# A mixture-of-experts encoder layer on one core: TensorE's order written out by hand from the third expert on

## The chip, the cores and the metric

One NeuronCore of a Trainium2 chip runs the whole program. The metric is the time of one execution on the device in microseconds (us), the median of the runs shown; a profiled execution is a run of its own. TensorE (PE in the profile, with its weight loads as PEld), VectorE (DVE), ScalarE (ACT), GpSimd (POOL) and SyncE (SP) each work through a queue of their own in order and wait for each other on semaphores.

## The reference

One encoder layer on 1024 tokens of width 1024 in float32: attention, a residual with layer norm, then a mixture of experts with 32 experts, four per token, and a second layer norm. What the change touches is the experts:

```
logits = x @ router_w + router_b
gates  = softmax(top 4 of the logits)
for each expert e, over the rows (tokens) that chose it:
    h = rows @ w_gate_up[e] + b_gate_up[e]              # 1024 -> 2048
    a = clamped_swiglu(h)                               # 2048 -> 1024
    y = a @ w_down[e]                                   # 1024 -> 1024
    out[token] += gate * (y + b_down[e])
x = layer_norm(alpha * x + out)
```

## The kernel before, in words

The attention stage (0 to about 530 us) and the router (to about 660 us) stand ahead of the experts and are not touched. The experts take most of the rest, to about 2045 us.

Experts run in an order e = 0 to 31. Each has a block of 128 rows; 18 of them, e = 1 to 8 and the even ones from 10 to 28 (`ovf(e)`, line 1132), have 32 overflow rows besides. The loop at the end of the stage calls, for each e, `gate_up(e)` (line 1212) and then `down(e - 1)` (line 1273), so the second product of an expert comes after the first product of the next.

A **weight piece** is a tile of 128 x 2048 float32 that SyncE fetches: eight for gate-up (called g0 to g7 below), four for down (d0 to d3). Products keep near float32 precision by splitting both factors into a high and a low part and adding three matmuls (`mm3`, all at line 55). So each piece is cast on ScalarE to `wh` (`prep_hi`, line 618) and its remainder `wl` is taken on VectorE (`prep_lo`, line 623), and TensorE then runs 12 matmuls of 128 x 512 on it. The tiles `wh` and `wl` come from a pool of three: the cast of piece n+3 can't start before TensorE has done its last read of piece n.

The stationary factor is the rows, transposed. For each expert `turn` (line 1144) lets TensorE transpose into the PSUM tile `tp` (line 1147), and `split` (lines 63 and 64) copies it out: ScalarE the high part, VectorE the low part, both reading `tp`. There is **one** `tp` tile (`ps_t`, `bufs=1`), so the next transposes wait until both have read it. The parts are, in one call of `gate_up(e)`: `turn_a(e-1, 0)` and `(e-1, 1)`, two halves of the activations of the expert before (`tpa`, four transposes each); `turn_a(e-1, 2)`, its overflow rows (`tpao`, two transposes, copied out by ScalarE alone), if it has any; and `turn_x(e+1, ...)`, the same three for the rows of the next expert (`tpx`, `tpx`, `tpxo`). `between` says after which piece of the gate-up each part stands in the program.

Overflow rows use TensorE in four strips of 32 columns: after piece g3 and after g7 a block of 16 float32 matmuls each (`go`), after d3 another (`yq`). The bias of gate-up is added by matmuls of `sel` with `b3` in bfloat16, four of 128 x 512 for `gu` and four of 32 x 512 for `go`, at the head of `gate_up`.

What sets the order: instructions are placed on each engine by a scheduler that works from estimated times, except inside `manual_schedule`, where the named engine keeps the order of the program. Before, TensorE is under it in `down` of experts with overflow rows only (line 1283). So in `gate_up` the scheduler moves transposes and biases about.

```python
            tp = ps_t.tile([P, 4, P], F32, tag="tp", name=f"tp{nm}")
            for c in range(nk):
                nc.tensor.transpose(tp[:, c, :], src[:, c * P:(c + 1) * P], ident)
            if lo is None:
                nc.scalar.copy(hi, tp[:, 0:nk, :])
            else:
                split(hi, lo, tp[:, 0:nk, :])
```

Of the kernel before, what the change touches and what calls it, by code (L numbers as in the profile page):

```python
# [20 lines left out]
P = 128  # L21
# [9 lines left out]
OVF = 32  # L31
# [14 lines left out]
def trunk_kernel(ctx: ExitStack, tc: tile.TileContext, x, w_qkv, q_norm, k_norm, w_o,  # L46
# [7 lines left out]
    def mm(o, lhsT, rhs, start=True, stop=True):  # L54
        nc.tensor.matmul(o, lhsT=lhsT, rhs=rhs, start=start, stop=stop)  # L55
# [525 lines left out]
    b3 = keep.tile([P, 2 * D], BF16, name="b3")  # L581
# [4 lines left out]
    sel = keep.tile([P, NE], BF16, name="sel")  # L586
# [461 lines left out]
    with tc.tile_pool(name="moex", bufs=1, side="right", reuse_waits="tile") as mx, \  # L1048
# [83 lines left out]
        def ovf(e):  # L1132
            return 1 <= RANK[e] <= NO
# [78 lines left out]
        def gate_up(e, between):  # L1212
            gus = [ps_g.tile([P, D], F32, tag=f"gu{h}", name=f"gu{e}_{h}") for h in range(2)]
            gu = [gus[n // 2][:, n % 2 * 512:(n % 2 + 1) * 512] for n in range(4)]
            if ovf(e):
                go = ps_o.tile([P, 512], F32, tag="o", name=f"go{e}")
            for n in range(4):
                sl = slice(n * 512, (n + 1) * 512)
                mm(gu[n], sel[:, e:e + 1].to_broadcast([P, P]), b3[:, sl], True, False)
            for n in range(4 if ovf(e) else 0):  # L1220
                mm(go[n * OVF:(n + 1) * OVF], sel[:, e:e + 1].to_broadcast([P, OVF]),
                   b3[:, n * 512:(n + 1) * 512], True, False)
            act[e], part, whole = swiglu(gus, D, e)
            by_cols = e in (0, NE - 1)
            later = []
            for k in range(KD - 2 if by_cols else KD):
                fetch(ci[0] + len(order))
                prep(ci[0] + 3)
                hi, lo, w = wts.pop((e, "g", k))
                xh, xl = xT[e][0][:, k, :], xT[e][1][:, k, :]  # L1230
                for n in range(4):
                    sl = slice(n * 512, (n + 1) * 512)
                    mm3(gu[n], xh, xl, hi[:, sl], lo[:, sl], False, k == KD - 1)
                later.append((k, w))
                if k % 4 == 4 - 1:
                    for kk, w in later if ovf(e) else ():
                        j, hf = divmod(kk, 2)
                        ts = slice(j * OVF, (j + 1) * OVF)
                        for n in range(4):
                            mm(go[n * OVF:(n + 1) * OVF], xoT[e][:, hf, ts], w[:, n * 512:(n + 1) * 512],  # L1240
                               False, kk == KD - 1)
                    later.clear()
                ci[0] += 1
                if k in between:
                    between[k]()
            if by_cols:

                end = []
                for k in range(KD - 2, KD):
                    fetch(ci[0] + len(order))  # L1250
                    prep(ci[0] + 3)
                    end.append((k, wts.pop((e, "g", k))))
                    ci[0] += 1
                for n in range(4):
                    sl = slice(n * 512, (n + 1) * 512)
                    for k, (hi, lo, w) in end:
                        mm3(gu[n], xT[e][0][:, k, :], xT[e][1][:, k, :], hi[:, sl], lo[:, sl], False, k == KD - 1)
                    if n == 0:
                        for k in (KD - 2, KD - 1):
                            if k in between:  # L1260
                                between[k]()
                    if n == 1:
                        part(0)
                part(1)
            else:
                whole()
            xT.pop(e)
            if ovf(e):
                xoT.pop(e)
                acto[e], _, whole = swiglu([go], 256, f"o{e}")  # L1270
                whole()

        def down(e, between={}):
            y = ys.pop(e, None) or mp.tile([P, D], F32, tag="y", bufs=2, name=f"y{e}")
            yp = ps_g.tile([P, D], F32, tag="gu0", name=f"yp{e}") if e == NE - 1 else \
                ps_y.tile([P, D], F32, tag="y", name=f"yp{e}")
            if ovf(e):
                yq = ps_o.tile([P, 512], F32, tag="o", name=f"yq{e}")
            ah, al = actT[e]
            later = []  # L1280
            in_turn = ExitStack()
            if ovf(e):
                in_turn.enter_context(tc.manual_schedule(engines={mybir.EngineType.PE}))
            for c in range(KD // 2):
                fetch(ci[0] + len(order))
                prep(ci[0] + 3)
                hi, lo, w = wts.pop((e, "d", c))
                for j in range(2):
                    k = 2 * c + j
                    for n in range(2):  # L1290
                        sl = slice(j * D + n * 512, j * D + (n + 1) * 512)
                        mm3(yp[:, n * 512:(n + 1) * 512], ah[:, k, :], al[:, k, :], hi[:, sl], lo[:, sl],
                            k == 0, k == KD - 1)
                later.append((c, w))
                if c == KD // 2 - 1:
                    for cc, w in later if ovf(e) else ():
                        ts = slice(cc * OVF, (cc + 1) * OVF)
                        for j in range(2):
                            for n in range(2):
                                sl = slice(j * D + n * 512, j * D + (n + 1) * 512)  # L1300
                                m = 2 * j + n
                                mm(yq[m * OVF:(m + 1) * OVF], actoT[e][:, j, ts], w[:, sl],
                                   cc == 0, cc == KD // 2 - 1)
                    later.clear()
                ci[0] += 1
                if c in between:
                    between[c]()
            in_turn.close()
            nc.scalar.mul(y, yp, gm_s[:, e:e + 1])  # L1309
            nc.gpsimd.indirect_dma_start(  # L1310
                out=fd, out_offset=bass.IndirectOffsetOnAxis(ap=mi[:, e:e + 1], axis=0),
                in_=y, in_offset=None, bounds_check=T + P - 1, oob_is_err=True, compute_op=ALU.add)
            if e == NE - 1:

                idle = ps_y.tile([P, D], F32, tag="y", name="idle")
                for r in range(22):
                    mm(idle[:, 0:512], ah[:, KD - 1, :], hi[:, 0:512])
            if not ovf(e):
                return
            H2 = 2 * OVF  # L1320
            ya = mp.tile([H2, 512], F32, tag="ya", bufs=1, name=f"ya{e}")
            nc.scalar.mul(ya, yq[H2:P], go_s[H2:P, e:e + 1])
            yo = mp.tile([H2, 512], F32, tag="yo", bufs=2, name=f"yo{e}")
            nc.vector.scalar_tensor_tensor(yo, yq[0:H2], go_s[0:H2, e:e + 1], ya, ALU.mult, ALU.add)
            nc.gpsimd.indirect_dma_start(
                out=fd2, out_offset=bass.IndirectOffsetOnAxis(ap=toh[:, e:e + 1], axis=0),
                in_=yo, in_offset=None, bounds_check=2 * (T + P) - 1, oob_is_err=True, compute_op=ALU.add)

        fetch(8)
        for e in range(NE):  # L1330
            between = {}
            if e > 0:
                for part in range(3):
                    between[part] = lambda part=part: turn_a(e - 1, part)
            if e + 1 < NE:
                if e == 0:
                    between[X1] = lambda: [turn_x(1, part) for part in range(3)]
                else:
                    for part in range(3):
                        between[(4 if e == 2 else 3) + part] = lambda part=part: turn_x(e + 1, part)  # L1340
            if e == 0:
                with tc.manual_schedule(engines={mybir.EngineType.DVE}):
                    slots(lambda: prep_lo(2))
            gate_up(e, between)
            if e == 1:
                list_blocks()
            if e + 2 < NE:
                gather_x(e + 2)
                gather_o(e + 2)
            if e == NE - 1:  # L1350
                between = {1 + part: lambda part=part: turn_a(NE - 1, part) for part in range(3)}
                down(e - 1, between)
            elif e > 0:
                down(e - 1)
        down(NE - 1)

    es_w.close()

# [161 lines left out]
```

## Time and profile before

| | us |
|---|---|
| median of 3 runs | 2085.25 (2083.95 to 2086.52) |
| the profiled execution's own time | 2086.0 |
| its span, first to last instruction | 2084.1 |
| TensorE busy in the span | 2031.2 |
| mean granted clock of TensorE | 0.993 |

Of a timeline row the first number is the start in us from the span's start, the second the duration. Matmuls are pipelined: a duration is longer than the distance to the next start, and it is the distances between starts that add up to the time. `LDWEIGHTS` on PEld loads the stationary factor of the matmul of the same name. In square brackets stands how long the engine was idle before, and what ended it. Buffer numbers are left out of names, so `tpx` is every `tpx`.

### The profile page before, as it was taken

Reading aid. Unit: us, or ns where it says so; the run is one execution under the profiler, and the core shown is the slowest. Engines: PE = TensorE matmul, PEld = TensorE weight load, DVE = VectorE, ACT = ScalarE, POOL = GpSimd, SP = SyncE. Lnnn points to the kernel's source line nnn. Section 1 sums busy time; section 2 is a strip of 40 time slices with the busy share of each in tenths; the row PEclk is TensorE's granted clock in tenths of the full one; section 3 lists DMA queues with packets and bytes.
Section 4 is the critical chain, followed back from the end, with each engine's and each line's share of the span. In section 5 each row is a group of like instructions: output and inputs, shape, how many; then the busy total and the mean of one; then the engine's idle time right before and its main releaser. Section 6 shows DMA issues by size and latency. Waiting matters only on the chain. (4 is left out here: it accounts for less than half of the span.)

```text
span 2084.1 us, 27850 instructions
## 1 busy us (share of the span) xinstructions
PE 2031.2 (97%) x10179; PEld 1374.0 (66%) x10179; DVE 1623.8 (78%) x1778; ACT 1292.0 (62%) x1566; POOL 534.8 (26%) x373
## 2 busy tenths in 40 slices
PE   8999999999997999999999999999999999999997
PEld 6774444444675666666667767767777677677774
DVE  6658778887888787776777878888778788887894
ACT  5656655565554656665666767667667676676774
POOL 1216676766134311121111102111011121011000
PEclk9999999999998999999999999999999999999999
DMA  5216000000545678778888988978989789789885
GB/s 173 71 61 178 31 31 21 31 21 11 201 153 205 261 287 304 279 284 295 291 300 333 361 304 317 366 288 349 334 319 372 291 330 355 284 345 340 325 319 182
DMA packets 106350, 500.38 MB, mean 240 GB/s; under 512 B 16002, under 2 KB 17027, under 8 KB 73443
## 3 DMA queue, kind: packets, MB, share of 16 engines
q1 hardware_dynamic: 87360, 447.02, 55.6%
q0 software_dynamic: 16000, 50.90, 8.9%
q8 instruction: 81, 1.33, 0.3%
q10 hardware_dynamic: 2850, 0.66, 0.2%
q14 instruction: 59, 0.48, 0.1%
HBM read 457.05 MB, written 41.49 MB: 239 GB/s over the span
## 5 line engine op out<-in xcount | busy, mean ns | idle before, releaser
L55 PE MATMUL gu<-wh,xTh 128*128 128x512 f32 x1024 | 415.0, 405 | 1.0 <-ACT xTh L63 1.0
L55 PE MATMUL gu<-wh,xTl 128*128 128x512 f32 x1024 | 409.9, 400 | 0.0
L55 PE MATMUL gu<-wl,xTh 128*128 128x512 f32 x1024 | 402.0, 394 | 0.2 <-DVE wl L623 0.2
L1310 POOL DMA_INDIRECT fd<-y,mi x32 | 79.1, 2473 | 655.6 <-ACT y L1309 655.6
L450 ACT ACTIVATE pt<-st 128x512 f32<-128x512 f32 x256 | 150.6, 597 | 134.9 <-PE st L55 109.6
L55 PEld LDWEIGHTS gu<-wh,xTh 128*128 128x128 f32 x1024 | 193.4, 189 | 42.5 <-ACT xTh L63 1.7
L55 PEld LDWEIGHTS gu<-wl,xTh 128*128 128x128 f32 x1024 | 193.1, 189 | 40.1 <-DVE wl L623 0.8
L55 PEld LDWEIGHTS gu<-wh,xTl 128*128 128x128 f32 x1024 | 193.5, 189 | 39.0 <-issue 3.6
L454 POOL TENSOR_TENSOR acc<-acc,pt 128x512 f32<-128x512 f32 x152 | 201.2, 1324 | 48.7 <-ACT pt L450 39.7
L55 PE MATMUL yp<-wl,aTh 128*128 128x512 f32 x512 | 204.3, 399 | 0.4 <-DVE wl L623 0.4
L55 PE MATMUL yp<-wh,aTh 128*128 128x512 f32 x512 | 201.6, 394 | 0.0
L55 PE MATMUL yp<-wh,aTl 128*128 128x512 f32 x512 | 199.7, 390 | 0.0
L440 DVE TENSOR_REDUCE nm<-sc 128x1 f32<-128x1024 f32 x124 | 150.4, 1220 | 29.2 <-PE sc L55 28.2
L55 PE MATMUL po<-pt,vn 128*64 128x512 f32 x512 | 135.7, 615 | 2.1 <-DVE ot L475 2.1
L609 POOL DMA_INDIRECT xg<-xd,mi x32 | 53.5, 1671 | 289.8 <-PE tpx L1147 281.7
L55 PE MATMUL qkv<-wh,xT 128*128 128x512 f32 x384 | 123.5, 402 | 2.6 <-ACT xT L63 1.4
L55 PE MATMUL st<-qs,kT_hi 128*128 128x512 f32 x256 | 116.6, 456 | 3.4 <-ACT pt L450 3.2
L55 PEld LDWEIGHTS yp<-wh,aTh 128*128 128x128 f32 x512 | 96.1, 188 | 33.5 <-ACT act L1191 14.2
L55 PEld LDWEIGHTS st<-qs,kT_hi 128*128 128x128 f32 x256 | 48.0, 187 | 97.7 <-ACT pt L450 66.9
L55 PEld LDWEIGHTS yp<-wl,aTh 128*128 128x128 f32 x512 | 96.3, 188 | 22.0 <-DVE wl L623 1.2
L55 PEld LDWEIGHTS yp<-wh,aTl 128*128 128x128 f32 x512 | 96.1, 188 | 19.6
L55 PE MATMUL st<-q,kT_lo 128*128 128x512 f32 x256 | 102.3, 400 | 0.6 <-DVE q L158 0.6
(523 smaller groups left out, 4209.4 us busy)
## 6 DMA issues: line engine op xcount, KB each, us to landing
w0g<-in_expert_w_gate_up SPq DMA_DIRECT2D x8, 1024.0 KB, 8.3
w1g<-in_expert_w_gate_up SPq DMA_DIRECT2D x8, 1024.0 KB, 7.7
w2g<-in_expert_w_gate_up SPq DMA_DIRECT2D x8, 1024.0 KB, 9.4
w3g<-in_expert_w_gate_up SPq DMA_DIRECT2D x8, 1024.0 KB, 7.0
w4g<-in_expert_w_gate_up SPq DMA_DIRECT2D x8, 1024.0 KB, 6.5
w5g<-in_expert_w_gate_up SPq DMA_DIRECT2D x8, 1024.0 KB, 6.7
w6g<-in_expert_w_gate_up SPq DMA_DIRECT2D x8, 1024.0 KB, 7.4
w7g<-in_expert_w_gate_up SPq DMA_DIRECT2D x8, 1024.0 KB, 7.8
```

The lines of the kernel that those rows point to most:

```text
L55: nc.tensor.matmul(o, lhsT=lhsT, rhs=rhs, start=start, stop=stop)
L440: nc.vector.tensor_reduce(nms[n][:, m:m + 1], sc.pop((n, m)), AX.X, ALU.max, negate=True)
L450: nc.scalar.activation(pts[n, k], st, AF.Exp)
L454: (nc.vector if k == 7 or n == NG - 1 or n == NG - 2 and k > 3 else nc.gpsimd).tensor_tensor(accs[n], pts[n, 0] if k == 1 else accs[n], pt ...
L609: return nc.gpsimd.indirect_dma_start(out=xg[e], out_offset=None, in_=xd, in_offset=bass.IndirectOffsetOnAxis(ap=mi[:, e:e + 1] if rows is ...
L1310: nc.gpsimd.indirect_dma_start(out=fd, out_offset=bass.IndirectOffsetOnAxis(ap=mi[:, e:e + 1], axis=0), in_=y, in_offset=None, bounds_chec ...
```

## The change

It puts TensorE under `manual_schedule` from the end of `gate_up(1)` to the end of `down(31)`, so that its instructions keep the program's order from expert 2 on. It moves the three parts of each `turn` in the program: from after pieces g0, g1, g2 (activations) to after g0, g2, g3, and from g3, g4, g5 (next rows; g4, g5, g6 in expert 2) to g4, g6, g7. And it moves the four `go` biases from the head of `gate_up` to just ahead of the first `go` block, behind g3. The work is the same, instruction by instruction.

```diff
-            for n in range(4 if ovf(e) else 0):
-                mm(go[n * OVF:(n + 1) * OVF], sel[:, e:e + 1].to_broadcast([P, OVF]),
-                   b3[:, n * 512:(n + 1) * 512], True, False)
             act[e], part, whole = swiglu(gus, D, e)
...
                 if k % 4 == 4 - 1:
+                    for n in range(4 if ovf(e) and k == 4 - 1 else 0):
+                        mm(go[n * OVF:(n + 1) * OVF], sel[:, e:e + 1].to_broadcast([P, OVF]),
+                           b3[:, n * 512:(n + 1) * 512], True, False)
                     for kk, w in later if ovf(e) else ():
...
-            in_turn = ExitStack()
-            if ovf(e):
-                in_turn.enter_context(tc.manual_schedule(engines={mybir.EngineType.PE}))
             for c in range(KD // 2):
...
-            in_turn.close()
...
         fetch(8)
+        in_turn = ExitStack()
         for e in range(NE):
             between = {}
             if e > 0:
-                for part in range(3):
-                    between[part] = lambda part=part: turn_a(e - 1, part)
+                for k, part in zip((0, 2, 3) if e > 1 else range(3), range(3)):
+                    between[k] = lambda part=part: turn_a(e - 1, part)
             if e + 1 < NE:
                 if e == 0:
                     between[X1] = lambda: [turn_x(1, part) for part in range(3)]
                 else:
-                    for part in range(3):
-                        between[(4 if e == 2 else 3) + part] = lambda part=part: turn_x(e + 1, part)
+                    for k, part in zip((4, 6, 7) if e > 1 else (3, 4, 5), range(3)):
+                        between[k] = lambda part=part: turn_x(e + 1, part)
...
             if e == 1:
                 list_blocks()
+
+                in_turn.enter_context(tc.manual_schedule(engines={mybir.EngineType.PE}))
...
         down(NE - 1)
+        in_turn.close()
```

On TensorE, in `gate_up(21)`, around the second half of the activations of expert 20 (`tpa20_1`; `wh250` and `wl250` are piece g2, `wh251` and `wl251` g3). Before:

```order
L55 MATMUL gu21_1_13317<-wl250_13328,xTh_21_13114 128x512
L55 MATMUL gu21_1_13317<-wh250_13326,xTh_21_13114 128x512
L1147 MATMUL tpa20_1_13370<-ident_70,act20_12998 128x128 x4
L55 MATMUL gu21_1_13317<-wh250_13326,xTl_21_13115 128x512
L55 MATMUL gu21_1_13317<-wl250_13328,xTh_21_13114 128x512
```

And now:

```order
L55 MATMUL gu21_1_13280<-wh250_13289,xTl_21_13096 128x512
L55 MATMUL gu21_1_13280<-wl250_13291,xTh_21_13095 128x512
L1147 MATMUL tpa20_1_13351<-ident_70,act20_12957 128x128 x4
L55 MATMUL gu21_0_13279<-wh251_13317,xTh_21_13095 128x512
L55 MATMUL gu21_0_13279<-wh251_13317,xTl_21_13096 128x512
```

Before, these transposes stand behind seven of the twelve matmuls of g2; now they stand behind all twelve. The overflow transposes `tpao20` stood behind seven matmuls of g3 and stand behind its twelfth now, with no other transposes between, and `tpxo22` likewise moves from within g6 to the end of g7, one piece behind `tpx22_1`, which moves from within g5 to the end of g6.

On ScalarE at the same place, the casts of g3 (`wh251`) to g6 (`wh254`) and the copies out of `tp` (`aTh`, and `aoT` for the overflow rows). Before:

```order
L618 CAST wh251_13354<-w21g3_13166 128x2048
L63 CAST aTh_20_13342<-tpa20_0_13345 128x512
L618 CAST wh252_13379<-w21g4_13184 128x2048
L63 CAST aTh_20_13342<-tpa20_1_13370 128x512
L618 CAST wh253_13411<-w21g5_13240 128x2048
L1149 COPY aoT20_13344<-tpao20_13395 128x256
L618 CAST wh254_13439<-w21g6_13258 128x2048
```

And now:

```order
L618 CAST wh251_13317<-w21g3_13122 128x2048
L63 CAST aTh_20_13305<-tpa20_0_13308 128x512
L618 CAST wh252_13335<-w21g4_13147 128x2048
L618 CAST wh253_13370<-w21g5_13203 128x2048
L63 CAST aTh_20_13305<-tpa20_1_13351 128x512
L618 CAST wh254_13392<-w21g6_13221 128x2048
L1149 COPY aoT20_13307<-tpao20_13386 128x256
```

The copy of the second half stood ahead of the cast of g5 and stands behind it now. VectorE follows: `aTl` of the second half stood ahead of `wl253` and stands behind it. At `tpx22_1` the same happens with the cast of piece d1 of expert 20 (`wh257`, `wl257`): it stands ahead of the copies of `tpx22_1` now. This is so in every odd `gate_up` from 9 to 29.

## Rows read from the trace of the kernel before

**Rows 1.** The page: TensorE over the span, and its granted clock in 40 slices.
```profile
PE 2031.2 (97%) x10179; PEld 1374.0 (66%) x10179; DVE 1623.8 (78%) x1778; ACT 1292.0 (62%) x1566; POOL 534.8 (26%) x373
...
PEclk9999999999998999999999999999999999999999
```

**Rows 2.** Stretch, length, busy of PE, PEld, DVE, ACT, POOL; PE clock; DMA share; GB/s.
```profile
1500.00:1600.00 100.00, 100.00 (x512) 73.42 (x510) 81.39 (x55) 68.42 (x51) 15.39 (x7) 1.00 0.90 338
```

**Rows 3.** Waits of the weight loads, 740 to 2045: total us, times, longest us.
```profile
PEld tpa L1147 <- DVE aTl L64: 9.9, 30, 0.5
PEld tpx L1147 <- DVE xTl L64: 7.2, 13, 3.2
```

**Rows 4.** TensorE's timeline, expert 19: transposes at the end of a piece (g0).
```profile
1501.96 0.39 PE L55 MATMUL gu<-wl,xTh 128*128 128x512 f32 x1
1502.19 0.60 PE L1147 MATMUL tpa<-ident,act 128*128 128x128 f32 x4
1502.55 0.48 PE L55 MATMUL gu<-wh,xTh 128*128 128x512 f32 x1
1502.86 0.40 PE L55 MATMUL gu<-wh,xTl 128*128 128x512 f32 x1
```

**Rows 5.** The same timeline: transposes within a piece (g2).
```profile
1506.76 0.39 PE L55 MATMUL gu<-wh,xTh 128*128 128x512 f32 x1
1507.05 0.66 PE L1147 MATMUL tpa<-ident,act 128*128 128x128 f32 x4
1507.46 0.48 PE L55 MATMUL gu<-wh,xTl 128*128 128x512 f32 x1
1507.77 0.39 PE L55 MATMUL gu<-wl,xTh 128*128 128x512 f32 x1
```

**Rows 6.** Timeline of all engines, expert 19, from the transposes behind g3 to the next.
```profile
1511.67 1.91 ACT L618 CAST wh<-w19g 128x2048 fp32r<-128x2048 f32 x1 [0.56 <-PE gu L55]
1511.71 0.60 PE L1147 MATMUL tpx<-ident,xg 128*128 128x128 f32 x4
...
1513.48 0.58 ACT L63 CAST xTh<-tpx 128x512 fp32r<-128x512 f32 x1
...
1513.61 2.29 DVE L623 TENSOR_TENSOR wl<-w19g,wh 128x2048 fp32r<-128x2048 f32 x1 [0.71 <-ACT wh L618]
...
1515.82 0.68 DVE L64 TENSOR_TENSOR xTl<-tpx,xTh 128x512 fp32r<-128x512 f32 x1
...
1516.56 0.20 PEld L1147 LDWEIGHTS tpx<-ident,xg 128*128 128x128 f32 x2 [0.35 <-DVE xTl L64]
```

**Rows 7.** TensorE's timeline, expert 20: `go`, transposes, one piece, transposes.
```profile
1552.10 3.64 PE L55 MATMUL go<-w20g,xoT 128*32 128x512 f32 x32
1555.67 0.66 PE L1147 MATMUL tpx<-ident,xg 128*128 128x128 f32 x4
...
1558.93 0.60 PE L1147 MATMUL tpx<-ident,xg 128*128 128x128 f32 x4
```

**Rows 8.** TensorE's timeline, expert 20: the `go` biases among the matmuls of g0.
```profile
1540.85 0.39 PE L55 MATMUL gu<-wh,xTh 128*128 128x512 f32 x1
1541.17 0.40 PE L55 MATMUL go<-b,sel 128*32 128x512 bf16 x4
1541.50 0.50 PE L55 MATMUL gu<-wh,xTl 128*128 128x512 f32 x1
1541.84 0.39 PE L55 MATMUL gu<-wl,xTh 128*128 128x512 f32 x1
```

**Rows 9.** TensorE's timeline: the waits of `tpx` in experts 1 and 2.
```profile
696.53 0.65 PE L1147 MATMUL tpx<-ident,xg 128*128 128x128 f32 x4 [1.30 <-DVE xTl L64]
...
768.21 0.66 PE L1147 MATMUL tpx<-ident,xg 128*128 128x128 f32 x4 [2.76 <-DVE xTl L64]
```

**Rows 10.** Stretches behind these two waits: columns as in rows 2.
```profile
696.50:698.00 1.50, 1.47 (x9) 1.13 (x10) 1.50 (x2) 0.97 (x3) 0.54 (x1) 1.00 0.13 52
...
769.50:772.50 3.00, 3.00 (x9) 2.36 (x8) 2.65 (x2) 2.11 (x2) 0.70 (x1) 0.51 0.50 130
```

## The prediction, before the changed kernel ran

> **What bounds the kernel now.** I read the page first, then the stretches, the waits, and the timeline row by row. TensorE is busy for 97% of the span and the clock is full in nearly every slice [rows 1]; among the experts a stretch of 100 us has TensorE busy for all of it at clock 1.00, with VectorE at 81, ScalarE at 68 and the DMAs at 0.90 [rows 2]. So the time of this stage is the sum of the distances between TensorE's starts. A plain 128 x 512 matmul takes 0.23 (1501.96 to 1502.19 [rows 4]), so a piece of twelve takes 2.72. Only what breaks this beat can be won, and every new wait of TensorE is lost in full. What breaks it: the weight loads of transposes wait a little for `aTl` or `xTl`, some 30 and 13 times [rows 3], because there is one `tp` tile and VectorE must have read it; a few microseconds in experts 1 and 2 [rows 9]; and the fixed cost of every change between kinds of matmul [rows 4, 5, 8].
>
> **What the change removes.** (1) *Transposes at the end of a piece.* At the end of g0 four transposes cost 0.90 from the start of the matmul before to that of the second behind; two matmuls are 0.45 of it, so they cost 0.45 [rows 4]. Within g2 it is 1.01, so 0.56, since the load waits [rows 5]. The late half now stands two pieces behind the first. 29 second halves of activations and 12 of rows pay this extra 0.11: 41 x 0.11 = **-4.5** (bounds: 0 to -6, if some overflow transposes gain as well).
>
> (2) *The `go` biases.* Among plain matmuls the four cost 0.99 - 0.45 = 0.54 [rows 8]: 0.09 above the beat on entry, 0.11 on exit, and 0.33 in between. At the head of the `go` block, which is in strips already, entry and exit fall away. 17 experts (2 to 8 and the ten even ones): 17 x 0.2 = **-3.4**. No row shows them joined; bounds are nothing won and all 0.54 won, 0 to -9. I stay near the entry and exit that the row shows.
>
> (3) *Expert 2's wait.* The second half of `tpx` waited 2.76 [rows 9], and behind it three microseconds ran at half clock [rows 10], which loses 1.5 more. Its cause is ScalarE, which stands behind a small DMA of the block list before it can copy `tp`. The change doesn't move that DMA much, but asks for `tp` about 1.1 later (two pieces, 24 matmuls, instead of 19), so I take off 1.1 and the half clock: **-2.5** (bounds 0 to -4.3).
>
> Joining `tpao` and `tpxo` to `go` blocks in experts 2 to 8 and parting `tpx` from them in 16 cases cancel to a few tenths. The `gu` biases stay four; TensorE pays the same for them wherever they stand.
>
> **What it adds.** The transposes are two pieces apart, but the overflow transposes follow after one. In expert 19 the profile shows what that costs. Transposes start at the end of a piece, 1511.71. At that same moment the last read of the piece frees a `wh` tile, so ScalarE has begun a cast of 1.91; the copy `xTh` follows at 1513.48. VectorE then takes `wl` for 2.2 and reaches `xTl` at 1515.82, which ends at 1516.50. The next transposes load at 1516.56: `tp` was held for 4.85 [rows 6]. A piece and the transposes ahead of it take 3.26 (1555.67 to 1558.93), 0.06 of that for standing behind a `go` block: 3.2 [rows 7]. Two pieces come to 5.9 and are safe. One piece is not: TensorE waits 4.85 - 3.2 = 1.65, and with the load that couldn't be made ahead (0.36 from transposes to the next matmul without a wait, 0.41 with one [rows 4, 5]) about **1.7**.
>
> Where are two `tp` users one piece apart? In experts 2 to 8 a `go` block of 3.6 (1552.10 to 1555.67 [rows 7]) stands between, and 6.8 is enough. In even gate-ups from 10 on the neighbours have no overflow rows. In the odd ones from 9 to 29 nothing stands between: `tpao` behind g3 follows the half behind g2, eleven times, and `tpxo` behind g7 follows the half behind g6, ten times (expert 30 has no overflow rows). In the order of the changed program the copy stands behind the cast there, on both engines, as in rows 6; before, the copy came first, because the transposes stood within the piece and ScalarE was idle. So 21 x 1.7 = **+35.7** (bounds 1.5 to 1.9 each: 31 to 40).
>
> Behind these waits ScalarE and VectorE have slack and nothing is late next. In the gate-ups of 29 and 30, where no `tpxo` wait stands ahead of `down`, one more `xTl` (0.68 [rows 6]) lies before the `wl` of the third down piece, which had been just in time: with the last expert's two halves, now a piece apart, I put these at **+2** (0 to 4).
>
> **The sum.** -4.5 - 3.4 - 2.5 + 35.7 + 2 = +27.3. Against the profiled execution's 2086.0 that is 2113.3; the median of the runs shown is 0.75 lower, so **2112.5**.
>
> The Trainium skill, "TensorE: Matmul & The Clock Gate", Part 2, says TensorE pulls weight loads ahead of running matmuls and keeps the matmuls themselves in order. Were it so here, those 0.05 would fall away, 21 x 0.05 = 1 off the sum; but in rows 6 it is the load of the waiting transposes itself that `xTl` releases, so I keep them.
>
> **Rivals.** *A, the waits also cost the clock.* An idle of 2.76 was followed by a stretch at 0.51 [rows 9, 10]. For it: 21 more idles, in pairs some 11 us apart (four pieces). Against it: the idle of 1.30, from the same kind of wait of the same length (it stretched the distance between two starts by the same 1.65), was followed by clock 1.00 [rows 9, 10]. If every wait lost 1.4 more: +29, **2142**. The same page, "A second HAM failure mode", says that TensorE idling briefly and often between groups can make its clock go up and down; no run shown here has idles so regular, and by that rule the time would be this rival's.
>
> *B, only one of the two kinds waits.* For the overflow rows of the next expert the hold hangs on what VectorE has in front of it at the end of gate-up; if it reached `xTl` 1.7 earlier there, ten waits would be gone and eleven left: 2112.5 - 10 x 1.7 = **2095**. Against it: the order has the cast and the `wl` first there as well.
>
> *C, faster: `tp` comes free in time.* If both engines served the transposes first, `tp` would be held for less than 3.2 and TensorE would wait for nothing; in expert 20 two halves stand one piece apart without a wait [rows 7], because casts had been done during the `go` block. Then only the gains are left: 2112.5 - 35.7 = **2077**. It decides at a hold of 3.2, and the sum passes zero at 3.6: without the waits it is -8.4, or 0.4 for each of the 21. Against it: each engine works in order, and the order has the cast first.
>
> *D, it comes out even*: the hold is near those 3.6, and **2085** stays.
>
> **Chances.** The forecast 0.74, A 0.12, B 0.07, C 0.05, D 0.02. With every term at its lower bound the sum is 31 - 6 - 9 - 4.3 + 0 = +12, at its upper 40 + 4 = +44, so 2097 to 2129; all at one end is unlikely, and the forecast's own range is 2100 to 2125. To hold 8 in 10 I reach down to B and leave out A and C: **2095 to 2125**. Within 0.2% (4 us, about what a measurement of this kernel can tell from no change): 0.02; faster 0.05; slower 0.93.
>
> **What would show it.** In the profile after: TensorE waiting for `aTl` ahead of `tpao` 11 times and for `xTl` ahead of `tpxo` 10 times, 1.3 to 1.7 each, in odd gate-ups from 9 on alone, and none of that between 780 and 1060 us; a distance of about 1.9 above the beat there; the clock at 1.00 through it; the second halves at 0.45; `go<-b` next to `go<-w`. The prediction is wrong if those transposes start on the beat, or if the granted clock in odd experts falls.

## The result, and the profile after

The changed kernel takes 2111.27 us (2110.78 to 2113.63, 4 runs), the kernel before 2085.32 (2083.95 to 2086.52, 4 runs): a ratio of 1.0124, 95% interval 1.0111 to 1.0136, or 26 us more. The sum of the prediction was +27.3, the forecast 2112.5. The profiled spans are 2109.2 and 2084.1, 25.1 apart.

The page of the changed kernel, as in [rows 1]:

```profile
PE 2023.7 (96%) x10179; PEld 1380.1 (65%) x10179; DVE 1622.9 (77%) x1778; ACT 1287.3 (61%) x1566; POOL 529.0 (25%) x373
...
PEclk9999999999998999999999999999999999999999
```

The work and the clock are the same; TensorE is busy 7.5 us less in a span that is 25.1 longer, so it stands idle more. Its waits from 740 to 2090 us in the changed kernel (engine, what waits, what ended it: total us, times, longest):

```profile
PE tpao L1147 <- DVE aTl L64: 16.6, 11, 1.5
PE tpxo L1147 <- DVE xTl L64: 15.0, 10, 1.5
...
PE yp L55 <- DVE wl L623: 1.4, 5, 0.4
PE tpx L1147 <- DVE xTl L64: 1.2, 1, 1.2
```

Eleven and ten waits of one length, on overflow transposes alone. One of them on the timeline of the changed kernel, all engines, in `gate_up(19)`:

```profile
1515.00 1.91 ACT L618 CAST wh<-w19g 128x2048 fp32r<-128x2048 f32 x1 [0.81 <-PE gu L55]
1515.03 0.60 PE L1147 MATMUL tpa<-ident,act 128*128 128x128 f32 x4
...
1516.81 0.58 ACT L63 CAST aTh<-tpa 128x512 fp32r<-128x512 f32 x1
1516.94 2.29 DVE L623 TENSOR_TENSOR wl<-w19g,wh 128x2048 fp32r<-128x2048 f32 x1 [0.43 <-ACT wh L618]
...
1517.99 0.39 PE L55 MATMUL gu<-wl,xTh 128*128 128x512 f32 x1
...
1519.15 0.68 DVE L64 TENSOR_TENSOR aTl<-tpa,aTh 128x512 fp32r<-128x512 f32 x1
1519.89 0.20 PEld L1147 LDWEIGHTS tpao<-ident,acto 128*128 128x128 f32 x2 [1.93 <-DVE aTl L64]
1519.89 0.44 PE L1147 MATMUL tpao<-ident,acto 128*128 128x128 f32 x2 [1.51 <-DVE aTl L64]
...
1520.08 0.48 PE L55 MATMUL gu<-wh,xTh 128*128 128x512 f32 x1
```

This is the chain of [rows 6], in another place: the transposes start as the last read of the piece frees a `wh` tile, ScalarE has begun its cast 0.03 earlier, `aTh` comes behind it, VectorE takes `wl` first, and `aTl` comes last. `tp` is held from 1515.03 to 1519.89, 4.86 us. The last matmul of the piece started at 1517.99 and its beat is 0.23, so the transposes come 1.67 behind it. With the transposes themselves such a place costs 1.95 to 1.98 above the beat at all 21 (counted from the start of the matmul ahead to the sixth behind), against 0.24 to 0.30 before.

The clock through that wait (columns as in [rows 2]):

```profile
1518.00:1519.80 1.80, 0.38 (x2) 0.00 (x0) 1.80 (x2) 1.61 (x1) 0.00 (x0) 1.00 0.98 366
1519.80:1522.00 2.20, 2.11 (x10) 1.78 (x11) 1.91 (x2) 0.66 (x2) 0.00 (x0) 1.00 1.03 426
```

In the first of them TensorE only finishes the matmuls of the piece (0.38 of 1.80); the granted clock is 1.00 there and behind it.

**Where the 25.1 us lie.** From the start of `gate_up(2)` to the first of the matmuls called `idle`, 22 without use for the result that follow `down(31)` in both kernels, the two take, by their timelines, first before and then changed:

```profile
740.15 1.04 PE L55 MATMUL gu<-b,sel 128*128 128x512 bf16 x4
...
2040.05 5.15 PE L55 MATMUL idle<-wh,aTh 128*128 128x512 f32 x22
```
```profile
741.30 1.04 PE L55 MATMUL gu<-b,sel 128*128 128x512 bf16 x4
...
2063.83 5.15 PE L55 MATMUL idle<-wh,aTh 128*128 128x512 f32 x22
```

1299.90 and 1322.53, so 22.6 more. The other 2.5 lie ahead of the part under the hand order (1.2) and behind it (1.3), in code that is the same. Behind it the granted clock differs, first before and then changed:

```profile
2040.05:2084.10 44.05, 29.93 (x89) 17.42 (x87) 20.78 (x46) 20.04 (x39) 1.55 (x1) 0.92 0.57 204
```
```profile
2063.83:2109.20 45.37, 30.57 (x89) 17.86 (x87) 20.88 (x46) 20.15 (x39) 1.55 (x1) 0.88 0.56 198
```

### The profile page after: what moved, and what is told of

Same layout as the page of the kernel before. It is cut to its first block, busy times and chain, and to the rows that moved or that the text cites. A ratio compares the mean times of both kernels' runs of the same rounds, so it can differ in the third digit from the quotient of the medians.

```text
span 2109.2 us, 27859 instructions
## 1 busy us (share of the span) xinstructions
PE 2023.7 (96%) x10179; PEld 1380.1 (65%) x10179; DVE 1622.9 (77%) x1778; ACT 1287.3 (61%) x1566; POOL 529.0 (25%) x373
## 5 line engine op out<-in xcount | busy, mean ns | idle before, releaser
L55 PE MATMUL gu<-wh,xTh 128*128 128x512 f32 x1024 | 421.1, 411 | 0.9 <-ACT xTh L63 0.9
L55 PE MATMUL gu<-wh,xTl 128*128 128x512 f32 x1024 | 400.3, 391 | 0.0
L55 PE MATMUL yp<-wl,aTh 128*128 128x512 f32 x512 | 200.0, 391 | 1.4 <-DVE wl L623 1.4
```

## The experiments

The kernel before ran beside each run: 2085.3 beside the changed kernel, 2086.6 beside runs 1 to 4, 2087.0 beside 5 to 8. A difference from the changed kernel, which ran in the first series alone, carries that 1 to 2 us. Between the two marks above, which leave out the code that is the same, the profiled executions of runs 1 to 8 took 1298.0, 1339.0, 1293.4, 1340.2, 1293.7, 1286.8, 1286.0 and 1348.3.

**1. Another PSUM tile for the overflow transposes.** The changed kernel, in which the overflow transposes of the odd gate-ups from 9 on use the `o` bank, idle there, instead of `tp`:

```diff
+            if spare:
+                tp = ps_o.tile([P, 512], F32, tag="o", name=f"tp{nm}").rearrange("p (c t) -> p c t", c=4)
+            else:
                 tp = ps_t.tile([P, 4, P], F32, tag="tp", name=f"tp{nm}")
...
-                turn(xo[e], xoT[e], None, 2, f"xo{e}")
+                turn(xo[e], xoT[e], None, 2, f"xo{e}", spare=e > 9 and not ovf(e - 1))
...
-                turn(acto[e], actoT[e], None, 2, f"ao{e}")
+                turn(acto[e], actoT[e], None, 2, f"ao{e}", spare=e + 1 >= 9 and not ovf(e + 1))
```

> The changed kernel, but in the odd gate-ups from 9 on the overflow transposes write to the PSUM tile of the overflow products, which is free there, instead of the one tile tp. Order and positions stay. Theory 1 (TensorE waits because the one tp tile is still being read): both kinds of wait go, 21 x 1.7 = 36 us; what comes next is the low part of down pieces d2 and d3, which is late in the even downs from 10 on as it is now in downs 28 and 29 alone, about 0.8 each, +8. So about 2111 - 36 + 8 = 2083. Theory 2 (ScalarE and VectorE are behind at these places, and any transposes of TensorE would meet that): the waits move by a piece but stay, and the time stays above 2100.

Measured: 2083.51, a ratio to the kernel before of 0.9983 (0.9973 to 0.9992). All 21 waits are gone, and the overflow transposes cost 0.24 each. So they were waits for the one tile, not for the data to be transposed and not a cost of the order as such. The 27.8 us won (24.5 between the marks) are less than 21 x 1.7 = 35.7. The rest stands for the most part in the waits of this run:

```profile
PE yp L55 <- DVE wl L623: 4.6, 15, 0.4
PE tpx L1150 <- DVE xTl L64: 2.4, 1, 2.4
```

Ten waits for a low part are new: with `tpxo` no longer waiting at the end of `gate_up`, VectorE is behind in the last piece of the even downs. Each takes some 0.6 above the beat, 6 us, and nine of these downs lose another 0.25 a piece earlier, 2 us. And the one wait of expert 2 is 2.4 long here instead of 1.2, with the clock at 0.64 and 0.50 in the two stretches behind it (769 to 770.5, 770.5 to 772.5): some 3 us. 35.7 less these 11 is close to the 24.5.

**2. The biases back at the head of `gate_up`**, with the hand order kept:

```diff
+            for n in range(4 if ovf(e) else 0):
+                mm(go[n * OVF:(n + 1) * OVF], sel[:, e:e + 1].to_broadcast([P, OVF]),
+                   b3[:, n * 512:(n + 1) * 512], True, False)
             act[e], part, whole = swiglu(gus, D, e)
...
-                    for n in range(4 if ovf(e) and k == 4 - 1 else 0):
-                        mm(go[n * OVF:(n + 1) * OVF], sel[:, e:e + 1].to_broadcast([P, OVF]),
-                           b3[:, n * 512:(n + 1) * 512], True, False)
```

> The changed kernel with the four overflow biases back at the head of gate_up, in the hand order. Theory 1 (a change between full matmuls and column strips costs about 0.2 on entry and exit, and the place at the go block saves it): in the changed kernel the four add 0.19 at the block; alone behind the gu biases they cost 0.52. So 17 x 0.33 = 5.6 slower than the changed kernel, about 2117. Rival (the biases' place doesn't matter, what changed is the transposes alone): 2111.

Measured: 2126.49, ratio 1.0190 (1.0173 to 1.0207), 15.2 above the changed kernel (16.4 between the marks); both theories were too low. The waits and the timeline of this run say why:

```profile
PE go L55 <- DVE yo L1320: 9.8, 16, 0.6
```
```profile
1557.59 1.04 PE L55 MATMUL gu<-b,sel 128*128 128x512 bf16 x4
1559.24 0.40 PE L55 MATMUL go<-b,sel 128*32 128x512 bf16 x4 [0.61 <-DVE yo L1320]
1559.57 0.50 PE L55 MATMUL gu<-wh,xTh 128*128 128x512 f32 x1
```

There is one `o` bank too. At the head of `gate_up` it still holds `yq` of the `down` just ended, and `yo` on VectorE (line 1320) has to read it first. Where nothing has to be read the four cost 0.56 among matmuls (0.54 by the starts in [rows 8], 0.56 counted to the sixth start behind), here 1.21: 1.02 more than the 0.19 at the head of the block, sixteen times 1.02 is 16. The scheduler of before had placed them a few matmuls into g0, where the bank was free. So under a hand order the move of the biases saves a wait that the kernel before did not have.

**3. More distance instead of a second tile.** In the odd gate-ups from 9 on the parts stand after g0, g2, g4 and g5, g7, and `tpxo` in the `down` behind, so that nothing stands one piece behind a half, which both engines copy; only the half after g5 is one piece behind `tpao`, which ScalarE alone copies:

```diff
-                for k, part in zip((0, 2, 3) if e > 1 else range(3), range(3)):
+                odd = e > 8 and e % 2
+                for k, part in zip((0, 2, 4) if odd else (0, 2, 3) if e > 1 else range(3), range(3)):
...
-                    for k, part in zip((4, 6, 7) if e > 1 else (3, 4, 5), range(3)):
+                    for k, part in zip((5, 7) if odd else (4, 6, 7) if e > 1 else (3, 4, 5), range(3)):
...
-                down(e - 1)
+                down(e - 1, {1: lambda: turn_x(e + 1, 2)} if odd else {})
```

> The changed kernel, with the parts in odd gate-ups from 9 on further apart and still at ends of pieces: activations after g0, g2, g4, next rows after g5 and g7, their overflow rows after d1 of the down that follows. No two users of tp are nearer than two pieces, but for the overflow activations, which ScalarE alone copies. Theory 1: no waits for tp, the low parts of d2 and d3 late by about 0.8 in all per odd expert: 2111 - 36 + 8 = 2083. Theory 2: the waits stay where VectorE is busiest, at the end of gate-up, 1 to 2 each: above 2095.

Measured: 2079.89, ratio 0.9963 (0.9949 to 0.9977). The 21 waits are gone with `tp` still one tile, and 14 waits for a low part are there, much as in the first run; one of them:

```profile
1527.09 0.39 PE L55 MATMUL yp<-wh,aTl 128*128 128x512 f32 x1
1527.80 0.50 PE L55 MATMUL yp<-wl,aTh 128*128 128x512 f32 x1 [0.32 <-DVE wl L623]
```

0.71 between two starts instead of 0.23, so 0.48, and 0.11 more behind it.

**4. The same fault put where there was none.** In the even gate-ups from 10 on the second half of the activations stands one piece behind the first instead of two:

```diff
-                for k, part in zip((0, 2, 3) if e > 1 else range(3), range(3)):
+                for k, part in zip((0, 1, 3) if e > 9 and ovf(e) else (0, 2, 3) if e > 1 else range(3), range(3)):
```

> The changed kernel, with one cause doubled: in the ten even gate-ups from 10 to 28 the second half of the activations stands after g1 instead of g2, one piece behind the first half. Theory 1: ten more waits of 1.65, 0.05 each for the late load: +17, about 2128. Theory 2 (only the places at g3 and g7 of the odd experts are short of VectorE): no new waits, 2111.

Measured: 2127.56, ratio 1.0193 (1.0176 to 1.0210), 16.3 above the changed kernel (17.6 between the marks). Waits of this run, and one on its timeline:

```profile
PE tpa L1147 <- DVE aTl L64: 14.9, 10, 1.5
```
```profile
1560.81 0.60 PE L1147 MATMUL tpa<-ident,act 128*128 128x128 f32 x4
...
1565.66 0.66 PE L1147 MATMUL tpa<-ident,act 128*128 128x128 f32 x4 [1.49 <-DVE aTl L64]
```

The hold is 4.85 again, and the transposes cost 2.17 instead of 0.47: 1.70 a wait, 17 for ten.

**5. The biases alone.** The kernel before, scheduler and all, with the `go` biases moved to just ahead of the first `go` block:

```diff
-            for n in range(4 if ovf(e) else 0):
-                mm(go[n * OVF:(n + 1) * OVF], sel[:, e:e + 1].to_broadcast([P, OVF]),
-                   b3[:, n * 512:(n + 1) * 512], True, False)
             act[e], part, whole = swiglu(gus, D, e)
...
                 if k % 4 == 4 - 1:
+                    for n in range(4 if ovf(e) and k == 4 - 1 else 0):
+                        mm(go[n * OVF:(n + 1) * OVF], sel[:, e:e + 1].to_broadcast([P, OVF]),
+                           b3[:, n * 512:(n + 1) * 512], True, False)
```

> The kernel before, with nothing changed but the place of the overflow biases: the 17 groups of four go<-b stand at the head of their expert's first go block, the scheduler still sets the rest. In the changed kernel a block with the biases at its head cost 3.98 us against 3.79 without them, so 0.19, where they cost 0.56 among the matmuls of before [rows 8]. T1: the saving is 0.37 x 17 = 6.3 us, so 0.997 of the time before, about 2080. T2 (the prediction's term): 0.2 x 17 = 3.4, 2083. T3: what the biases covered turns into a wait for a low part, the time does not move.

Measured: 2080.57, ratio 0.9972 (0.9962 to 0.9982), so 4 to 8 us, at the middle 5.8. The first theory fits. Joined to the block the four cost this (timeline of this run):

```profile
1880.52 0.40 PE L55 MATMUL go<-b,sel 128*32 128x512 bf16 x4
1880.74 3.61 PE L55 MATMUL go<-w28g,xoT 128*32 128x512 f32 x32
```

0.22 from their start to the block's, against the 0.33 plus entry and exit of [rows 8]. The four are not faster by themselves: they run side by side, and all four take 0.40 in either place, as long as one full-width matmul (0.39). What the strips behind them save beyond entry and exit is 0.11 of those 0.33, which seems to have belonged to the change of kind too.

In the profiled execution (6.2 less between the marks) the wait of expert 2 was as long as before, but the clock behind it stayed at full:

```profile
768.26 0.66 PE L1147 MATMUL tpx<-ident,xg 128*128 128x128 f32 x4 [2.82 <-DVE xTl L64]
```
```profile
768.20:772.00 3.80, 3.42 (x16) 2.57 (x16) 2.69 (x3) 3.48 (x3) 1.07 (x1) 1.00 0.26 50
```

That is worth some 1.6 of the 6.2; two new short waits in expert 2, 0.8 together, go the other way. So the price of the biases is surer from its rows than from this difference.

**6. Work laid over the late low parts.** The third run, and three of the four `gu` biases of the next expert but one put into the last piece of each even down from 8 on. The diff shows the place alone; left out are the third run's edits and the new function `biases`, which holds the calls that stood at the head of `gate_up`:

```diff
-                        mm3(yp[:, n * 512:(n + 1) * 512], ah[:, k, :], al[:, k, :], hi[:, sl], lo[:, sl],
-                            k == 0, k == KD - 1)
+                        o = yp[:, n * 512:(n + 1) * 512]
+                        mm(o, ah[:, k, :], hi[:, sl], k == 0, False)
+                        mm(o, al[:, k, :], hi[:, sl], False, False)
+                        if 8 <= e < NE - 2 and e % 2 == 0 and k == KD - 2 and n == 0:
+                            biases(e + 2, range(3))
+                        mm(o, ah[:, k, :], lo[:, sl], False, k == KD - 1)
```

> The run with the spread transposes (2079.89), and in addition three of the four gate-up biases of the next expert but one put into the last weight piece of every even down from 8 on, between the second matmul and the first that reads the low part, where the scheduler of before had put two. In that run PE stood 0.48 us at this place, ten times, for DVE's subtraction wl. T1: the waits were a price of the hand order, which has no work left to lay over a late low part; the biases cover them and cost there what they cost anyway: 11 x 0.5 = 5.5 us less, about 2074. T2: DVE is what lags, and the next low part is late instead, 2080.

Measured: 2075.29, ratio 0.9942 (0.9928 to 0.9955), 4.6 below the third run (6.5 between the marks). On its timeline:

```profile
1523.82 0.39 PE L55 MATMUL yp<-wh,aTl 128*128 128x512 f32 x1
1524.05 0.82 PE L55 MATMUL gu<-b,sel 128*128 128x512 bf16 x3
1524.53 0.58 PE L55 MATMUL yp<-wl,aTh 128*128 128x512 f32 x1
```

The low part is in time behind the biases, and three such waits are left in downs. VectorE did not lag: it was only late by 0.5 at one place of each even down.

**7. Expert 2 as well.** The sixth run, with `tpx` of expert 2 after g4 and g7:

```diff
-                    for k, part in zip((5, 7) if odd else (4, 6, 7) if e > 1 else (3, 4, 5), range(3)):
+                    for k, part in zip((4, 7) if e == 2 else (5, 7) if odd else (4, 6, 7) if e > 1 else (3, 4, 5), range(3)):
...
-                down(e - 1, {1: lambda: turn_x(e + 1, 2)} if odd else {})
+                down(e - 1, {1: lambda: turn_x(e + 1, 2)} if odd or e == 2 else {})
```

> As the run with the three biases filled in, and for expert 2 the second half of the next rows' transposes after g7 instead of g6 and its overflow in the down behind, since the pair at 768 us cost 1.9 to 2.3 us there against 0.46. T1: 1.5 to 1.8 us less than that run, and 1.5 more where the clock had fallen, about 2072. T2: the ScalarE queue, held up by a DMA at this place, is late for the weight pieces as well, the same time as that run.

Measured: 2072.17, ratio 0.9931 (0.9918 to 0.9945), 14.8 below the kernel before in the same series (2086.97). No transposes wait any more, and two stretches of it read

```profile
1500.00:1600.00 100.00, 100.00 (x513) 74.65 (x512) 83.66 (x59) 68.45 (x50) 14.73 (x7) 1.00 0.91 349
762.00:775.00 13.00, 13.00 (x76) 8.54 (x76) 9.47 (x9) 7.23 (x6) 1.28 (x1) 1.00 0.70 236
```

This version beats both kernels. It is 3.1 below the sixth, more than the 1.8 expected, but that is not the edit's doing alone. The profiled executions are 3.8 apart; between the marks they differ by 0.9, and 2.7 lie ahead of expert 2, in code that is the same. The idle of 1.4 is gone, and a low part that is late now in the `down` that holds the overflow transposes takes part of it back, 0.66 above the beat:

```profile
781.01 0.39 PE L55 MATMUL yp<-wh,aTl 128*128 128x512 f32 x1
781.77 0.50 PE L55 MATMUL yp<-wl,aTh 128*128 128x512 f32 x1 [0.37 <-DVE wl L623]
```

**8. No distance at all.** The changed kernel with the second half of `tpx` directly ahead of `tpxo`, after g7, in the odd gate-ups from 9 on:

```diff
-                    for k, part in zip((4, 6, 7) if e > 1 else (3, 4, 5), range(3)):
-                        between[k] = lambda part=part: turn_x(e + 1, part)
+                    for k, part in zip((4, 7, 7) if e > 8 and e % 2 else (4, 6, 7) if e > 1 else (3, 4, 5), range(3)):
+                        between[k] = lambda p=part, f=between.get(k): (f and f(), turn_x(e + 1, p))
```

> The changed kernel with the distance taken away: in the odd gate-ups from 9 on the second half of the next rows stands directly ahead of their overflow transposes, after g7. T1 (a wait is the hold of the one tp tile less the distance to its next writer, and the clock stays): the distance falls from 3.2 to 0.35, each of the ten waits grows by 2.9 to about 4.5 us, 2111.3 + 10 x 2.9 = 2140. T2 (a longer wait also drops TensorE's clock, as the idle of 2.8 us at 768 did in the kernel before, where 1.5 us more were lost): 2140 + 10 x 1.5 = 2155 and more, with a granted clock below 0.99 in windows behind the waits. T3 (the wait is set by a date, not by the hold): 2111.

Measured: 2135.36, ratio 1.0237 (1.0221 to 1.0252), 24.1 above the changed kernel. Neither number was right, and both theories had half of it. The timeline of one place and the stretches at it, in this run:

```profile
1543.08 0.60 PE L1147 MATMUL tpx<-ident,xg 128*128 128x128 f32 x4
1546.21 0.69 PE L1147 MATMUL tpxo<-ident,xo 128*128 128x128 f32 x2 [2.53 <-DVE xTl L64]
1546.55 0.78 PE L55 MATMUL yp<-wh,aTh 128*128 128x512 f32 x1
1547.12 0.63 PE L55 MATMUL yp<-wh,aTl 128*128 128x512 f32 x1
```
```profile
1543.50:1546.00 2.50, 0.17 (x2) 0.00 (x0) 2.44 (x3) 2.49 (x3) 1.80 (x1) 0.96 1.01 419
...
1547.00:1549.00 2.00, 2.00 (x6) 1.52 (x6) 2.00 (x2) 0.30 (x1) 1.05 (x1) 0.50 0.98 395
```

The hold is 3.13 here and not 4.86: behind g7 only ScalarE's cast stood ahead of the copies, and VectorE had no `wl` to take between `xTh` and `xTl`. And behind the 2.53 us of idling the clock is at 0.50. Six matmuls from 1546.55 to 1549.24 take 2.69 instead of 6 x 0.23 = 1.4, so 1.3 a wait is lost to the clock. The pair of transposes costs 4.62 above the beat, against 0.46 + 1.95 in the changed kernel: 2.2 each, 22 for ten. In expert 2 the idle was 1.85 here instead of 1.22, with the clock down behind it, some 2 more.

## Why the prediction was right, and where it was not

**The waits** (+35.7, 21 x 1.7). Right in number, place and size: eleven `tpao` and ten `tpxo`, in the odd gate-ups from 9 on, none in experts 2 to 8, each 1.70 above what it cost before (1.97 against 0.27). The hold of 4.85 read from one place [rows 6] came back as 4.86 in the changed kernel and 4.85 in run 4. Runs 1 and 3 take the waits away by two different means, and run 4 makes ten more of the same price. Of the rivals, B (one kind alone) and C (`tp` free in time) fall with the table of waits, and D (a hold near 3.6) with the 4.86. The weight load that cannot be made ahead was also as put: the transposes that waited cost 0.19 to the next matmul (1519.89 to 1520.08), those of the third run that didn't 0.13 (1509.03 to 1509.16). The Trainium skill, "TensorE: Matmul & The Clock Gate", Part 2, has loads pulled ahead of running matmuls; here the load of the waiting transposes started with them, at 1519.89.

**The clock** (rival A, 0.12). It stayed, through 21 idles of 1.5 us in the changed kernel and 31 in run 4. But run 8 shows that the rival was not far: there ten idles are 1.0 longer, each followed by 0.50. And the ground on which it was set aside, that an idle of 1.30 kept the clock and one of 2.76 did not, was thin: the idle of 2.82 in run 5 kept it too. That 21 idles of 1.5 would all keep it was right, but two single idles did not show it beforehand. The stretch that holds all these waits, first in the changed kernel, then in run 8:

```profile
1070.00:1990.00 920.00, 887.90 (x4601) 646.56 (x4601) 725.25 (x488) 594.20 (x427) 126.94 (x61) 1.00 0.85 318
```
```profile
1070.00:1990.00 920.00, 878.06 (x4482) 642.11 (x4475) 709.34 (x477) 579.28 (x417) 130.84 (x60) 0.98 0.83 313
```

The Trainium skill, "TensorE: Matmul & The Clock Gate", "A second HAM failure mode", has short, frequent idles between groups making the clock oscillate; the changed kernel doesn't show it, and run 8, whose idles are longer, has the clock fall behind ten of them and come back each time.

**The biases** (-3.4). Right in sign, and mis-sized. I took off the entry and exit of [rows 8] alone. The four cost 0.19 at the head of the block and not 0.33, so the saving is 0.56 - 0.19 = 0.37 each, 6.3 for 17; run 5, with nothing else changed in the program, measured 5.8 (4 to 8).

**Second halves at a piece's end** (-4.5). As put: 0.57 to 0.60 within a piece, 0.45 to 0.48 now.

**Expert 2** (-2.5). The transposes cost 1.9 there instead of 3.4, with an idle of 1.2 instead of 2.76, and the 1.6 lost at half clock are gone: about -3.1. Part of this is luck. The idle is not a fixed number: 2.76 and 2.82 with the scheduler's order (run 5), 1.22 to 2.42 in the changed kernel and the six runs that ask for `tp` at the same place; their mean is 1.6, so the 1.1 that I took off is about right and the changed kernel drew the shortest. The half clock behind it came back in runs 1 and 8 and was missing in run 5. What moves the two stays open.

**The late low parts** (+2). Five places at 0.47 to 0.58, in downs 28 and 29 and the last gate-up: about +2.5. What I missed is that the same lateness lay under the waits of all even downs: the idle ahead of `down` gave VectorE its time, so the 21 waits cost 35.7 as they stood, and taking them away gave 6 (run 3) to 8 (run 1) less.

**The sum.** 35.7 - 6.3 - 4.5 - 3.1 + 2.5 = 24.3, against 22.6 between the two marks. The joining of `tpao` and `tpxo` to `go` blocks in experts 2 to 8, which I let cancel, is about -1 of the difference: there each expert gained 0.65, of which 0.37 + 0.11 are the biases and one half. That the forecast missed by only 1.2 is in part luck, errors that cancel: the biases too small by 2.9 on one side, and on the other 2.5 us outside the hand order that no step foresaw, half of them beside a lower clock (0.88 against 0.92) at the end.

The three gains were real all along: 6.3 + 4.5 + 3.1 = 13.9, and run 7, which has them without the 21 waits, is 14.8 below the kernel before, 13.9 between the marks. That the two agree so well is chance: run 7 also has no wait at all in expert 2, and low parts that are late.

## What to carry to other kernels

Where one buffer is passed between engines, put its hold time beside the distance to its next user, read the hold from a place where the copying engines are in the phase that the new order gives them, and give each pair of users that distance; here a piece (3.2) fell short of 4.85 and two did not. An order written by hand takes away the scheduler's choice of what to lay over a small lateness: after the change look for operands that had been just in time, and put loose work such as biases there. Small matmuls that use the array in strips are best put next to others that do, as the biases here, where the bank that they write is free (run 2).

## What the runs showed of the hardware that was not expected

A wait of TensorE can have a second price. In three kernels (the changed one, runs 2 and 4) 21 or 31 idles of about 1.5 us a run left the granted clock at 1.00; ten of 2.53 us were each followed by matmuls at half clock (1.2 of 2.4 GHz), six of them in 2.69 us, which cost another 1.3. The length of the idle does not decide it alone. In expert 2 idles of 2.42 and 2.76 were followed by stretches at 0.50 and 0.51 and one of 1.85 (run 8) by one at 0.63, those of 1.22 to 1.66 by 1.00, but one of 2.82 (run 5) by 1.00 as well. What else decides stays open here. Four bf16 matmuls of 32 columns cost 0.56 between full-width ones and 0.19 at the head of a block in strips.
